# Sums over partitions by the tensor engine, taken 32 columns wide instead of one or two

## The chip, the cores and the metric

The kernel runs on one core of one Trainium2 chip. The metric is the time on the device in microseconds (us), the median of several runs. One more execution of each kernel is taken with the hardware profiler. The engines are named as the profile names them: PE is the tensor engine (PEld its weight loads), DVE the vector engine, ACT the scalar engine, POOL GpSimd, SP the engine that issues most of the DMAs.

## What is computed

The reference puts two transformer blocks behind one another, on 512 tokens of width 1024, all in float32. Cut to what matters here:

```python
# block 1
mod = silu(c) @ mod_w + mod_b                      # six vectors of 1024
h = rmsnorm(x, norm1_g) * (1 + sc1) + sh1          # a sum over 1024 features for each token
x = x + g1 * (mixed(h) @ w_out)                    # attention with forget gates, and pooling
h = rmsnorm(x, norm2_g) * (1 + sc2) + sh2
x = rmsnorm(x + g2 * conv_ffn(h), final_g)
# block 2
h = rms_norm(x, ln1_g); proj = h @ w_in
aq, ak = rms_norm(heads(aq), q_norm_g), rms_norm(heads(ak), k_norm_g)   # a sum over 64 features of a head
attn = rms_norm(neighbourhood_attention(aq, ak, av), attn_out_g)
dn = rms_norm(gated_delta_rule(l2_norm(q), l2_norm(k), v, ...), out_norm_g) * silu(z)   # sums over 128 features of a head
x = x + concat([attn, dn]) @ w_out
x = x + hierarchical_moe(rms_norm(x, ln2_g), ...)  # 64 experts, two for each token
```

## The kernel before

Up to the end of the mixer of the second block, activations lie with features on the 128 partitions and the 512 tokens along the free axis (`xT` is eight tiles of 128x512). A sum over features is then a sum over partitions, and the tensor engine takes it: a 128x128 piece of the squares is loaded as weights, a column of ones is streamed through it, and the result is one column of PSUM with a token's sum on each partition. Four such matmuls cover 512 tokens. In float32 one matmul of the program is two instructions of PE, each with its own weight load.

These places take such sums. `gemv_done` (L268 to L275) turns the accumulated products of a modulation vector into eight columns. `shift_share` (L277 to L289) does it for the shift's share of a projection, two columns. `ColSums.done` (L308 to L312) does it for squares that POOL has added up, `ColSumsPE.done` (L327 to L333) for squares that PE has added up into 32 equal rows of four quarters; there the column is `w32`, which holds 1/32. `head_norm` (L726 to L748) uses a selector of two columns (`hsel`), one for each head of 64 features. `dn_q_out` (L1033 to L1041) and `scan_out` (L1188 to L1209) take sums over the 128 features of a head. Behind each a DVE instruction reads the few columns from PSUM, mostly followed by a power -1/2 on POOL and, where the row is needed along the free axis, by four transposes on PE (`row_bcast`, L348).

The big projections are matmuls of 128x512 at L177 to L179 (three products of split fp32 operands); between the projections stand the attention heads (L485, L508, L526), the levels of a triangular inverse (`levels`, L1079 to L1111, its 128-column matmuls at L1098) and the scan (L1153 to L1186). From about 1060 us on the experts run, with their matmuls at L1728 and L1757.

The order of PE's instructions is fixed when the program is built: a planner orders the work of each engine by its place in the code, readiness and its own costs, save where `manual_schedule` pins PE's order (the attention heads, the router and the experts). So a sum can stand among matmuls of a projection or of an attention head, and `gemv_done` of a vector can run long before the code's last user of it.

Of the kernel before, what the change touches and what calls it, by code (L numbers as in the profile page):

```python
# [9 lines left out]
F32 = mybir.dt.float32  # L10
# [4 lines left out]
AF = mybir.ActivationFunctionType  # L15
ALU = mybir.AluOpType
# [5 lines left out]
EPS = 1e-6  # L22
# [67 lines left out]
def hybrid_kernel(ctx, tc, A, out, dbg=None):  # L90
    nc = tc.nc
# [7 lines left out]
    cp = pool("const")  # L99
# [8 lines left out]
    vec = cp.tile([128, _NV], F32, name="vec")  # L108
    cst = cp.tile([128, _NC], F32, name="cst")

    def V(name, i=0, n=1):
        o, _ = _VEC[name]
        return vec[:, o + i:o + i + n]

    def C(name):
        if name in _CST:
            o, n = _CST[name]
            return cst[:, o:o + n]
        o, n = _CST2[name]
        return cst2[:, o:o + n]  # L120

    ident = C("ident")
    ones32 = cp.tile([128, 32], F32, name="ones32")
    w32 = cp.tile([128, 1], F32, name="w32")
    zb = cp.tile([128, 128], BF16, name="zb")
    nhalf = cp.tile([128, 8], F32, name="nhalf")
    modT = cp.tile([128, 48], F32, name="modT")
    gs = cp.tile([128, 16], F32, name="gs")
    nc.vector.memset(ones32, 1.0)
    nc.vector.memset(w32, 1.0 / 32.0)  # L130
    nc.gpsimd.memset(zb, 0.0)
    nc.vector.memset(nhalf, -0.5)

# [134 lines left out]
    def gemv_done(u, acc):  # L268

        if acc is None:  # L270
            return
        p = ps("gv", "gvt")
        for j in range(8):
            nc.tensor.matmul(p[:, j:j + 1], acc[j // 4][:, j % 4 * 128:j % 4 * 128 + 128], ones32[:, 0:1], start=True, stop=True)
        nc.vector.tensor_tensor(modT[:, u * 8:u * 8 + 8], p[:, 0:8], V("mod_b", u * 8, 8), op=ALU.add)  # L275

    def shift_share(w_raw, sh0, pool):  # L277

        sw = pool.tile([128, 256], F32, name="sw")
        for k in range(8):  # L280
            sk, wk = modT[:, sh0 + k:sh0 + k + 1], w_raw[k // 4][:, k % 4, :]
            if k == 0:
                nc.vector.tensor_scalar(sw, wk, sk, None, op0=ALU.mult)
            else:
                nc.vector.scalar_tensor_tensor(sw, wk, sk, sw, op0=ALU.mult, op1=ALU.add)
        p = ps("gv", "pqb")
        for m in range(2):
            nc.tensor.matmul(p[:, m:m + 1], sw[:, m * 128:m * 128 + 128], ones32[:, 0:1], start=True, stop=True)
        return p  # L289


    class ColSums:
# [15 lines left out]
        def done(self):  # L308
            pt = ps(self.tag, "cst")
            for t in range(4):  # L310
                nc.tensor.matmul(pt[:, t:t + 1], self.a[:, t * 128:t * 128 + 128], ones32[:, 0:1], start=True, stop=True)
            return pt[:, 0:4]  # L312

    class ColSumsPE:

# [10 lines left out]

        def done(self):  # L327
            part = sp_.tile([128, S], F32, tag="tmp", name="part", bufs=4)
            nc.scalar.activation(part, self.p, AF.Copy)
            pt = ps(self.tag, "cst")  # L330
            for t in range(4):
                nc.tensor.matmul(pt[:, t:t + 1], part[:, t * 128:t * 128 + 128], w32, start=True, stop=True)
            return pt[:, 0:4]  # L333

    def col_sums(srcs, tag="pc"):
        cs = ColSumsPE(len(srcs), tag)
# [257 lines left out]
    with ExitStack() as st:  # L594
# [13 lines left out]
        for m in range(2):  # L608
            a = fp.tile([128, S], F32, tag="act", name="a_first", bufs=2)
# [6 lines left out]
        for third, n in enumerate((8, 8, 6)):  # L616
            ah, al = [], []
            for jj in range(n):
                j = off + jj
                if j == 7:  # L620
                    gemv_done(5, acc5)
                p = proj(A["wup"][j], hh, hl, tag=("pb", "mm")[j % 2]) if j else p_first
                cv = []
                for m in range(2):
                    ci = j + 22 * m
                    c = fp.tile([128, S], F32, tag=f"cv{m}", name=f"cv{m}", bufs=2)
# [99 lines left out]
    def head_norm(pp, gain):  # L726

        pt = ps("pa", "hn")
        aa = []
        for m in range(2):  # L730
            a = slot("cv", "a", 6)
            nc.scalar.activation(a, pp[m], AF.Copy, scale=gain)
            aa.append(a)
            sq = slot("cv", "sq", 6)
            nc.scalar.activation(sq, pp[m], AF.Square)
            for t in range(4):
                o = m * 8 + t * 2
                nc.tensor.matmul(pt[:, o:o + 2], sq[:, t * 128:t * 128 + 128], C("hsel"), start=True, stop=True)
        v, r = (sp_.tile([128, 2] + d, F32, tag=f"hn{i}", name="hnv", bufs=1 + i) for i, d in enumerate(([4, 2], [2, 4])))
        pv = pt[:, 0:16].rearrange("p (m t e) -> p m t e", m=2, t=4)  # L740
        for m in range(2):
            nc.vector.tensor_tensor(v[:, m], pv[:, m], rr2.unsqueeze(2).to_broadcast([128, 4, 2]), op=ALU.mult)
        nc.vector.tensor_scalar(v, v, 1.0 / 64, EPS, op0=ALU.mult, op1=ALU.add)
        for m in range(2):
            nc.gpsimd.tensor_tensor(v[:, m], v[:, m], nhalf.rearrange("p (t e) -> p t e", t=4), op=ALU.pow)
            nc.vector.tensor_tensor(r[:, m].rearrange("p e t -> p t e"), v[:, m], rr.unsqueeze(2).to_broadcast([128, 4, 2]),
                                    op=ALU.mult)
        return aa, r  # L748
# [284 lines left out]
    def dn_q_out(c):  # L1033
        for h in (2 * c, 2 * c + 1):
            sq = tmp("sq")
            nc.scalar.activation(sq, qT[h], AF.Square)
            pt = ps("pb", "pqs")
            for t in range(4):
                nc.tensor.matmul(pt[:, t:t + 1], sq[:, t * 128:t * 128 + 128], ones128[:, 0:1], start=True, stop=True)
            nc.vector.tensor_scalar(qs[:, h * 4:h * 4 + 4], pt[:, 0:4], 128 * EPS, 128 * EPS * EPS,  # L1040
                                    op0=ALU.mult, op1=ALU.add)  # L1041

    vT = {}
# [144 lines left out]
    def scan_out(po, tag):  # L1188
        pt = ps(tag, "pst")
        a = sp_.tile([128, 2, 4], F32, tag="sa", name="sa", bufs=1)  # L1190
        r = sp_.tile([128, 2, 4], F32, tag="sr", name="sr", bufs=1)
        h0 = min(po)
        da = {}
        for h in po:
            so, da[h] = tmp("so"), tmp("da")
            nc.scalar.activation(so, po[h], AF.Square)
            nc.vector.scalar_tensor_tensor(da[h], po[h], V("dng"), zs[h], op0=ALU.mult, op1=ALU.mult)
            for t in range(4):
                i = (h - h0) * 4 + t
                nc.tensor.matmul(pt[:, i:i + 1], so[:, t * 128:t * 128 + 128], ones128[:, 0:1], start=True, stop=True)  # L1200
        nc.vector.scalar_tensor_tensor(a, pt[:, 0:8].rearrange("p (h t) -> p h t", h=2), 1.0 / 128,
                                       qs[:, h0 * 4:h0 * 4 + 8].rearrange("p (h t) -> p h t", h=2),
                                       op0=ALU.mult, op1=ALU.add)
        nc.gpsimd.tensor_tensor(r, a, nhalf.rearrange("p (h t) -> p h t", h=2), op=ALU.pow)
        for h in po:
            R = row_bcast(r[:, h - h0], "pb")
            nc.vector.tensor_tensor(da[h], da[h], R, op=ALU.mult)
            new_mix2(4 + h)
            split_h(mixh[4 + h], mixl[4 + h], da[h])  # L1209
# [715 lines left out]
```

## Time and profile before

| | us |
|---|---|
| median of 3 runs | 1554.95 |
| lowest and highest run | 1553.94, 1559.04 |
| profiled execution, its own time | 1553.21 |
| profiled execution, span from the first to the last instruction | 1551.3 |

PE is busy 95% of the span, DVE 54%, ACT 33%, POOL 16%. The mean granted clock of PE is 0.972 of its full speed. In the page's 40 slices a granted clock below full speed stands in the first slices, around the middle of the span and at the change to the experts. The chain that ended last lies on PE for 76% of the span.

"Granted clock" is the clock that PE was allowed in a stretch, as a share of 2.4 GHz; 0.5 is 1.2 GHz. In a timeline row the first number is the start in us from the start of the span, the second the time from the first start to the last end of the instructions that the row merges. Ends of matmuls are modelled and a matmul's row holds its way through the array, so that the step from one start to the next tells more of its cost than its duration.

### The profile page before, as it was taken

What the parts mean: (1) busy time and instruction counts of PE and PEld (TensorE: products, weight loads), DVE (VectorE), ACT (ScalarE), POOL (GpSimd) and SP (SyncE); (2) the same over time, 40 slices, a digit from 0 to 9 for tenths busy, and PEclk for the clock granted to TensorE, in tenths of its full rate; (3) what the DMA queues carried; (4) which work ended last, traced back from release to release, by engine and by line L of the source; (5) the groups of instructions that cost most, each with busy time, mean ns of one, the idle gap of its engine ahead of it and who ended that gap; (6) DMA issues with size and microseconds to landing.
All of it is one profiled execution on the core that took longest, in us unless ns stands there. A gap on an engine that the chain in (4) does not pass through costs nothing.

```text
span 1551.3 us, 20448 instructions
## 1 busy us (share of the span) xinstructions
PE 1467.0 (95%) x7500; PEld 1012.8 (65%) x7500; DVE 842.6 (54%) x1724; ACT 516.1 (33%) x981; POOL 251.6 (16%) x317
## 2 busy tenths in 40 slices
PE   6899999999999999998889999997999999999997
PEld 3766686888888887876667788884444444444443
DVE  3778776653564457266797666564333333233234
ACT  4554434441442345254334434422311111111111
POOL 0242021000000004323562330102100000000000
PEclk9989999999999999998989999997999999999999
DMA  8753143332222223353333131567999999999995
GB/s 334 244 201 122 60 145 109 103 101 94 96 96 95 95 82 99 101 171 102 85 116 77 30 92 50 196 220 295 421 418 424 425 423 424 424 424 424 423 424 185
DMA packets 82573, 327.69 MB, mean 211 GB/s; under 512 B 18086, under 2 KB 21798, under 8 KB 58144
## 3 DMA queue, kind: packets, MB, share of 16 engines
q1 hardware_dynamic: 80736, 321.63, 55.4%
q0 software_dynamic: 1728, 4.66, 0.8%
q8 instruction: 61, 1.00, 0.3%
q14 instruction: 48, 0.39, 0.1%
HBM read 319.42 MB, written 8.47 MB: 211 GB/s over the span
## 4 chain that ended last, share of the span: by engine, by line
PE 76%; DVE 10%; DMA 4%; issue 3%; POOL 3%; ACT 2%; SPq 1%; DVEq 0%; POOLq 0%; ACTq 0%
PE pgu L1728 14%; PE pj L177 10%; PE pj L179 10%; PE pj L178 10%; PE pd L1757 7%; PE pkept L1775 2%; PE pkept L1776 2%; PE pcmb L1775 2%; PE pcmb L1776 2%; DVE wlo L171 2%; DMA graw<-in_modw_dram 1%; DVE cv L875 1%; PE pS L485 1%; DMA xg<-xs,tok_of 1%; DVE E L950 1%
## 5 line engine op out<-in xcount | busy, mean ns | idle before, releaser
L177 PE MATMUL pj<-hh,whi 128*128 128x512 f32 x640 | 259.2, 406 | 16.1 <-ACT cn L869 7.7
L179 PE MATMUL pj<-hh,wlo 128*128 128x512 f32 x640 | 257.2, 403 | 4.8 <-DVE wlo L171 4.8
L178 PE MATMUL pj<-hl,whi 128*128 128x512 f32 x640 | 257.1, 402 | 0.5 <-DVE hl L200 0.5
L1728 PE MATMUL pgu<-wgu,xw 128*64 128x512 f32 x1024 | 227.1, 596 | 0.1
L171 DVE TENSOR_TENSOR wlo<-wraw,whi 128x1024 fp32r<-128x1024 f32 (+4 forms) x122 | 148.4, 1218 | 47.6 <-ACT whi L170 44.5
L170 ACT ACTIVATE whi<-wraw 128x1024 fp32r<-128x1024 f32 (+4 forms) x122 | 125.0, 1027 | 136.3 <-PE pj L178 119.2
L1728 PEld LDWEIGHTS pgu<-wgu,xw 128*64 128x64 f32 x1024 | 70.4, 137 | 139.3 <-issue 137.9
L177 PEld LDWEIGHTS pj<-hh,whi 128*128 128x128 f32 x640 | 123.5, 193 | 48.8 <-ACT cn L869 10.2
L179 PEld LDWEIGHTS pj<-hh,wlo 128*128 128x128 f32 x640 | 123.7, 194 | 34.6 <-DVE wlo L171 5.3
L178 PEld LDWEIGHTS pj<-hl,whi 128*128 128x128 f32 x640 | 123.8, 193 | 26.0 <-issue 1.2
L1734 DVE SCALAR_TENSOR_TENSOR hid<-pgu,agt,sg 128x256 f32<-128x256 f32 x32 | 15.5, 484 | 194.0 <-ACT sg L1732 194.0
L1732 ACT ACTIVATE sg<-pgu,agt 128x256 f32<-128x256 f32 x32 | 15.2, 476 | 305.1 <-PE pgu L1728 305.1
L1757 PE MATMUL pd<-wd,hT 128*64 128x512 f32 x512 | 115.5, 593 | 0.4 <-ACT xgT L1580 0.4
L1779 DVE TENSOR_TENSOR xr<-xr,pcmb 128x512 f32<-128x512 f32 x128 | 82.2, 683 | 28.7 <-PE pcmb L1776 28.7
L306 POOL TENSOR_TENSOR acc<-acc,sq 128x512 f32<-128x512 f32 x21 | 33.7, 1623 | 391.6 <-ACT sq L305 391.3
L198 DVE SCALAR_TENSOR_TENSOR og<-pd,agt,og 128x512 fp32r<-128x512 f32 x64 | 48.0, 750 | 79.6 <-ACT og L194 79.6
L1719 POOL COPY xw<-xgT 128x512 f32 x56 | 32.9, 616 | 353.8 <-PE pgu L1728 343.7
L1757 PEld LDWEIGHTS pd<-wd,hT 128*64 128x64 f32 x512 | 36.2, 137 | 72.3 <-issue 63.1
L179 PE MATMUL pj<-ah,wlo 128*128 128x512 f32 x176 | 69.3, 394 | 0.0
L177 PE MATMUL pj<-ah,whi 128*128 128x512 f32 x176 | 69.3, 394 | 0.0
L178 PE MATMUL pj<-al,whi 128*128 128x512 f32 x176 | 69.3, 394 | 0.0
L194 ACT ACTIVATE og<-pd,agt 128x512 fp32r<-128x512 f32 x64 | 44.0, 688 | 75.3 <-PE pd L1757 74.2
(455 smaller groups left out, 2630.3 us busy)
## 6 DMA issues: line engine op xcount, KB each, us to landing
wgu<-in_egu_dram SPq DMA_DIRECT2D x128, 1024.0 KB
wd<-in_ed_dram SPq DMA_DIRECT2D x62, 1024.0 KB
graw<-in_modw_dram SPq DMA_DIRECT2D x48, 512.0 KB
wraw<-in_wup_dram SPq DMA_DIRECT2D x42, 512.0 KB
wraw<-in_win_dram SPq DMA_DIRECT2D x38, 512.0 KB
wraw<-in_wdn_dram SPq DMA_DIRECT2D x20, 512.0 KB
wraw<-in_wout_dram SPq DMA_DIRECT2D x16, 512.0 KB
E<-gscr SPq DMA_DIRECT2D x16, 256.0 KB
```

The costliest lines, as they stand in the source:

```text
L170: nc.scalar.activation(hi, raw, AF.Copy)
L171: nc.vector.tensor_tensor(lo, raw, hi.bitcast(F32), op=ALU.subtract)
L177: nc.tensor.matmul(p, whi, hh, start=first, stop=False)
L178: nc.tensor.matmul(p, whi, hl, start=False, stop=False)
L179: nc.tensor.matmul(p, wlo, hh, start=False, stop=last)
L194: nc.scalar.activation(hi, src, AF.Identity, scale=scale, bias=0.0 if bias is None else bias)
L198: nc.vector.scalar_tensor_tensor(lo, src, scale, hi.bitcast(F32), op0=ALU.mult, op1=ALU.subtract)
L1728: nc.tensor.matmul(gu[64 * i:64 * i + 64, :], xw[:, j, 64 * i:64 * i + 64], wts.gu[e][j], start=(j == 0), stop=(j == 7))
L1757: nc.tensor.matmul(pd[64 * i:64 * i + 64, :], hT[:, j, 64 * i:64 * i + 64], wts.d[e][:, j, n * 512:n * 512 + 512], start=(j == 0), stop=(j ...
L1775: nc.tensor.matmul(pc, OT[:, ts], a, start=(n == 1 or start), stop=False, skip_group_check=(n == 0))
L1776: nc.tensor.matmul(pc, OT[:, ts], b, start=False, stop=(n == 1 or stop), skip_group_check=(n == 0))
L1779: nc.vector.tensor_tensor(v, v, pc, op=ALU.add)
```

## The change

All sums over partitions named above stream 32 equal columns instead of one: `ones32`, a 128x32 tile of ones that was there, takes the place of its own first column, of the first column of `ones128`, and of `w32`, which is removed with its memset. The scale 1/32 of `w32` moves into the copy on ACT ahead of it. The selector of two columns is repeated 16 times by its access pattern. Each sum now has 32 columns of PSUM instead of one, and a new helper, `wide`, gives the readers a view of every 32nd column. Number and order of the matmuls in the code stay as they were.

```diff
+    def wide(p, n):
+        return p[:, 0:32 * n].rearrange("p (n c) -> p n c", c=32)[:, :, 0]
...
-    w32 = cp.tile([128, 1], F32, name="w32")
...
-    nc.vector.memset(w32, 1.0 / 32.0)
...
 # gemv_done
-            nc.tensor.matmul(p[:, j:j + 1], acc[j // 4][:, j % 4 * 128:j % 4 * 128 + 128], ones32[:, 0:1], start=True, stop=True)
-        nc.vector.tensor_tensor(modT[:, u * 8:u * 8 + 8], p[:, 0:8], V("mod_b", u * 8, 8), op=ALU.add)
+            nc.tensor.matmul(p[:, 32 * j:32 * j + 32], acc[j // 4][:, j % 4 * 128:j % 4 * 128 + 128], ones32, start=True, stop=True)
+        nc.vector.tensor_tensor(modT[:, u * 8:u * 8 + 8], wide(p, 8), V("mod_b", u * 8, 8), op=ALU.add)
...
 # shift_share
-            nc.tensor.matmul(p[:, m:m + 1], sw[:, m * 128:m * 128 + 128], ones32[:, 0:1], start=True, stop=True)
-        return p
+            nc.tensor.matmul(p[:, 32 * m:32 * m + 32], sw[:, m * 128:m * 128 + 128], ones32, start=True, stop=True)
+        return wide(p, 2)
...
 # ColSums.done
-                nc.tensor.matmul(pt[:, t:t + 1], self.a[:, t * 128:t * 128 + 128], ones32[:, 0:1], start=True, stop=True)
-            return pt[:, 0:4]
+                nc.tensor.matmul(pt[:, 32 * t:32 * t + 32], self.a[:, t * 128:t * 128 + 128], ones32, start=True, stop=True)
+            return wide(pt, 4)
...
 # ColSumsPE.done
-            nc.scalar.activation(part, self.p, AF.Copy)
+            nc.scalar.activation(part, self.p, AF.Copy, scale=1.0 / 32)
...
-                nc.tensor.matmul(pt[:, t:t + 1], part[:, t * 128:t * 128 + 128], w32, start=True, stop=True)
-            return pt[:, 0:4]
+                nc.tensor.matmul(pt[:, 32 * t:32 * t + 32], part[:, t * 128:t * 128 + 128], ones32, start=True, stop=True)
+            return wide(pt, 4)
...
 # head_norm
-                o = m * 8 + t * 2
-                nc.tensor.matmul(pt[:, o:o + 2], sq[:, t * 128:t * 128 + 128], C("hsel"), start=True, stop=True)
+                o = (m * 4 + t) * 32
+                nc.tensor.matmul(pt[:, o:o + 32], sq[:, t * 128:t * 128 + 128],
+                                 C("hsel").unsqueeze(1).to_broadcast([128, 16, 2]), start=True, stop=True)
...
-        pv = pt[:, 0:16].rearrange("p (m t e) -> p m t e", m=2, t=4)
+        pv = pt[:, 0:256].rearrange("p (m t c) -> p m t c", m=2, t=4)[:, :, :, 0:2]
...
 # dn_q_out
-                nc.tensor.matmul(pt[:, t:t + 1], sq[:, t * 128:t * 128 + 128], ones128[:, 0:1], start=True, stop=True)
-            nc.vector.tensor_scalar(qs[:, h * 4:h * 4 + 4], pt[:, 0:4], 128 * EPS, 128 * EPS * EPS,
+                nc.tensor.matmul(pt[:, 32 * t:32 * t + 32], sq[:, t * 128:t * 128 + 128], ones32, start=True, stop=True)
+            nc.vector.tensor_scalar(qs[:, h * 4:h * 4 + 4], wide(pt, 4), 128 * EPS, 128 * EPS * EPS,
...
 # scan_out
-                nc.tensor.matmul(pt[:, i:i + 1], so[:, t * 128:t * 128 + 128], ones128[:, 0:1], start=True, stop=True)
-        nc.vector.scalar_tensor_tensor(a, pt[:, 0:8].rearrange("p (h t) -> p h t", h=2), 1.0 / 128,
+                nc.tensor.matmul(pt[:, 32 * i:32 * i + 32], so[:, t * 128:t * 128 + 128], ones32, start=True, stop=True)
+        nc.vector.scalar_tensor_tensor(a, wide(pt, 8).rearrange("p (h t) -> p h t", h=2), 1.0 / 128,
```

## Rows read from the trace of the kernel before

**Rows 1.** The page: span, busy time by engine, the chain by engine

```profile
span 1551.3 us, 20448 instructions
...
PE 1467.0 (95%) x7500; PEld 1012.8 (65%) x7500; DVE 842.6 (54%) x1724; ACT 516.1 (33%) x981; POOL 251.6 (16%) x317
...
PE 76%; DVE 10%; DMA 4%; issue 3%; POOL 3%; ACT 2%; SPq 1%; DVEq 0%; POOLq 0%; ACTq 0%
```

**Rows 2.** PE's groups by line and shape: count | busy us, mean ns | idle before

```profile
L738 PE MATMUL hn<-cst,sq 128*128 128x2 f32 x64 | 9.5, 270 | 5.8 <-ACT sq L735 5.7
...
L984 PE MATMUL kk<-kT 128*128 128x128 f32 x32 | 4.3, 276 | 0.0
L551 PE MATMUL ppool<-ud,pw 128*128 128x512 f32 x8 | 4.1, 592 | 0.0
```

**Rows 3.** Timeline of PE, 842 to 856 us: start, us, line, count

```profile
845.75 1.06 PE L1098 MATMUL lvW<-U,DD 128*128 128x128 f32 x8
846.77 1.05 PE L1039 MATMUL pqs<-ones,sq 128*128 128x1 f32 x8
...
848.40 1.05 PE L1039 MATMUL pqs<-ones,sq 128*128 128x1 f32 x8
849.31 1.55 PE L1098 MATMUL lvY<-DD,U 128*128 128x128 f32 x8
850.65 1.92 PE L1098 MATMUL lvQ<-YY,NX 128*128 128x128 f32 x8
```

**Rows 4.** Stretches: PE, PEld, DVE, ACT, POOL busy; granted clock, DMA share, GB/s

```profile
621.20:624.60 3.40, 2.89 (x22) 2.38 (x20) 1.39 (x4) 0.00 (x0) 2.05 (x2) 1.00 0.00 0
624.60:628.00 3.40, 3.40 (x10) 2.72 (x10) 2.48 (x5) 0.04 (x1) 2.93 (x11) 0.50 0.60 192
...
846.40:849.80 3.40, 3.40 (x28) 2.90 (x27) 1.60 (x5) 2.12 (x6) 1.84 (x2) 1.00 0.35 124
849.80:853.20 3.40, 3.40 (x18) 3.40 (x18) 2.57 (x4) 1.19 (x2) 0.21 (x1) 0.51 0.00 0
853.20:856.60 3.40, 3.40 (x31) 3.11 (x30) 2.50 (x4) 0.00 (x0) 0.53 (x1) 0.99 0.00 0
```

**Rows 5.** Timeline of PE, 618 to 650 us, at the sums of L311

```profile
622.08 1.05 PE L311 MATMUL cst<-ones,acc 128*128 128x1 f32 x8 [0.51 <-POOL acc L306]
...
623.78 0.95 PE L311 MATMUL cst<-ones,acc 128*128 128x1 f32 x8
624.59 0.77 PE L178 MATMUL pj<-hl,whi 128*128 128x512 f32 x1
```

**Rows 6.** Timelines of PE at four idle gaps; in brackets the idle time before

```profile
18.38 1.11 PE L351 MATMUL rb<-cst,rsr 128*128 128x128 f32 x4 [2.32 <-POOL rsr L345]
...
94.70 0.70 PE L485 MATMUL pS<-kT,zq 64*128 64x256 f32 x2 [2.51 <-DVE mx L493]
...
95.77 2.98 PE L274 MATMUL gvt<-ones,gacc 128*128 128x1 f32 x14
...
243.56 1.05 PE L311 MATMUL cst<-ones,acc 128*128 128x1 f32 x8 [2.32 <-POOL acc L306]
...
708.88 1.87 PE L738 MATMUL hn<-cst,sq 128*128 128x2 f32 x8 [5.20 <-ACT sq L735]
```

**Rows 7.** Stretches as in rows 4, behind the four gaps

```profile
17.00:24.00 7.00, 5.62 (x52) 2.90 (x56) 1.54 (x2) 0.00 (x0) 1.32 (x1) 0.51 1.03 411
...
95.00:106.00 11.00, 11.00 (x38) 7.60 (x36) 5.78 (x31) 4.63 (x12) 2.30 (x2) 0.53 0.56 206
...
245.00:250.00 5.00, 5.00 (x18) 4.02 (x17) 2.28 (x4) 1.34 (x2) 0.92 (x1) 0.66 0.00 0
...
710.00:720.00 10.00, 10.00 (x32) 8.44 (x33) 4.55 (x11) 2.22 (x5) 4.84 (x11) 0.50 0.37 92
```

**Rows 8.** DVE's reads of PSUM behind transposes (L229) and sums (L275), by line and shape

```profile
L229 DVE TENSOR_TENSOR modT<-gvt,vec 128x8 f32<-128x8 f32 x3 | 0.5, 166 | 2.4 <-PE gvt L226 2.4
...
L275 DVE TENSOR_TENSOR modT<-gvt,vec 128x8 f32<-128x8 f32 x3 | 0.5, 160 | 1.3 <-PE gvt L274 1.3
```

## The prediction

> **What bounds the kernel now.** I read the page first, for the engine that the chain follows: the tensor engine (PE) is busy 95% of the 1551.3 us and carries 76% of the chain that ended last [rows 1]. So a microsecond taken from or given to PE in a stretch where it has no idle time moves the end by about as much, and what a slower engine beside it does is mostly cover. I read next the groups of PE instructions by line and shape, for what the edited matmuls cost today: 64 instructions at L738 [rows 2], and by the same view 48 at L274, 32 each at L1039, L1200 and L311, 8 each at L332 and L288, 224 in all. Each fp32 matmul of the program is two instructions, so 112 matmuls. Last I read the timeline and the stretches around each group of sums, for what they wait for, how far apart they start, and above all at which granted clock PE runs before and after them.
>
> The reader should see two things there. A sum of one column is not cheap: eight instructions at L1039 start at 846.77 us and what follows the second such group starts 0.91 us after it (848.40 to 849.31) [rows 3], that is about 0.11 us an instruction, the same step as eight instructions with 128 columns (lvW, 845.75 to 846.77, 1.02 us) [rows 3]. And the clock falls right behind sums: in 846.4 to 849.8 us PE is busy all of 3.40 us at a granted clock of 1.00, in the next 3.40 us it is still busy all the time, and the granted clock is 0.51 [rows 4], the lower of its two levels, 1.2 GHz against 2.4 GHz. The sums of the two normalisations before the second block (L311) show the same: two groups from 622.08 to 624.59 [rows 5], granted clock 1.00 in 621.2 to 624.6 and 0.50 in 624.6 to 628.0 [rows 4].
>
> **The change part by part.**
>
> *The width itself.* 224 instructions stream 32 columns instead of one (two at L738). The trace has one-column and two-column sums and 128-column matmuls with the same 128x128 fp32 weights, and 32 lies between. By means, the 128-column L984 takes 276 ns and the two-column L738 270 ns [rows 2]: 6 ns for 126 columns. The step from start to start is the same 0.11 us for both [rows 3]. So the weight load sets the step and the columns run under it: cost of the step 0, lower bound 0 (nothing is taken out that could give time), upper bound below under the rivals. What is left is that the last matmul of a group ends later for its reader. There are 20 places where a reader waits (by the code three vectors of the modulation, two shift shares, five normalisations, four head norms, four query sums, two of the scan). At 6 ns each that is 0.1 us, at the slope between L984 and the 512-column L551 (592 less 276 ns over 384 columns, 0.82 ns a column, 31 columns, 26 ns) [rows 2] it is 0.5 us. I take 0.1 us, since 128 columns is the nearer row.
>
> *The readers.* DVE now reads every 32nd column of the bank instead of neighbours. The trace has both ways on the same shape: L229 reads every 32nd column of a bank and takes 166 ns, L275 reads neighbours and takes 160 ns [rows 8]. Cost 6 ns at most a place, counted at 0. Bounds 0 to 0.1 us over 20 places.
>
> *Moved arithmetic and the removed tile.* The 1/32 goes from the column of weights into the scale of a copy that ScalarE makes anyway, and a memset at the start goes; neither is on the chain, which enters the start by the loads of x. If that cover is gone they cost or give under 0.1 us. No DMA, queue or wait is added, and no instruction is added to or taken from PE. The two-column selector (L738) becomes a repeated read of the same two columns. I cost it as a 32-column read. No row shows such a narrow repeat as a moving operand, so its bounds are those of the width.
>
> *The clock.* This is the only term of size. A fall costs what its stretch loses: 3.40 us busy at 0.51 does 1.73 us of full-speed work, a loss of 1.67 us, and 3.40 us at 0.50 loses 1.70 us [rows 4]. The rows around the first one check it: the groups that start at 849.31 and 850.65 us show 1.55 and 1.92 us against 1.06 us for lvW before [rows 3], 1.35 us on two groups with a third still slow. Which falls would go? In six places low clock stands beside sums. At two of them the sums are what PE does before the fall: at 846.77 to 849.3 us there is no idle time at all, at 622.08 to 624.59 us there is 0.51 us [rows 3, 5]. There the columns that pass rise most, so there I let the fall go: 1.67 + 1.70 = 3.37 us. At the other four a real gap of PE comes first: 2.32 us ahead of 18.38, 2.51 us ahead of 94.70, 2.32 us ahead of 243.56 and 5.20 us ahead of 708.88 us [rows 6]. A few wider sums don't fill a gap, so I let these stay. Bounds of the clock term: 0 to all six. PE is busy without a break in both low stretches [rows 4], and what is late next is PE itself, so the gain isn't taken by another engine at once.
>
> The Trainium skill, page "TensorE: Matmul & The Clock Gate", section "Why this matters for your kernels", puts falls of the clock down to idle gaps of PE between bursts of matmuls. By that alone the stretch before 849.8 us, which has none, would not fall, and wider sums would save nothing. The row differs: the clock falls there, so I go by the row. By the page the sum is +0.1 us, by the rows -3.3 us.
>
> *Sum.* -3.37 + 0.1 = -3.27 us on the profiled execution's 1553.21 us (span 1551.3 and 1.9 around it), 1549.9 us. The median of the runs shown, 1554.95, stands 1.74 us above that execution, so the median is forecast at 1551.7 us.
>
> **The rivals.**
>
> *B, the columns don't count enough.* The falls at 624.6 and 849.8 us stay, or as many come elsewhere. For it: 32 columns under a step that has room for 128 is still mostly weight loading. Against it: 853.2 to 856.6 us, as full of small matmuls with as many weight loads but of 128 columns, keeps a granted clock of 0.99 [rows 4], and the stretch that fell differs from it by its narrow sums. Time: +0.1 to +0.5 us, 1555.1 to 1555.5.
>
> *C, more falls go.* The stretches behind the gaps shrink too. Losses there: 17 to 24 us at 0.51, 3.4 us; 95 to 106 at 0.53, 5.2; 245 to 250 at 0.66, 1.7; 710 to 720 at 0.50, 5.0 [rows 7], 15.3 us together. For it: after 95.77 and 708.88 us the sums themselves run at the low clock (eight instructions take 1.87 us) [rows 6] and may be what holds it there. Against it: the gaps. With a typical one of these, 3.4 us, on top of the forecast: -6.7 us, 1548.3; with all, 1536.4.
>
> *D, the columns are not hidden.* If the weight load can't run beside the matmul before it, each instruction grows by 31 columns at 0.82 ns, 26 ns [rows 2], over 224 instructions 5.7 us, and PE is the bound. Then the change is slower: 1560.7 if the falls stay, 1557.4 if the two go. It decides from 15 ns an instruction on, where the cost passes the 3.37 us saved. The place to see it is the four head norms (L738), 64 instructions. Against it stand the equal steps of one and 128 columns [rows 3]. The Trainium skill, same page, section "Part 3: Packing small matmuls", says that weights load beside a running matmul only when the row groups differ, which here they don't; by that D would hold. The trace disagrees: the step stays 0.11 us with 128 columns.
>
> *E, the order of PE changes.* The program's order on PE is fixed when it is built, by a plan that weighs costs: the first modulation sums stand in the code behind all four head pairs (L580) and run among the logits of the first at 95.77 us [rows 6]. A sum that the plan takes for longer may be put elsewhere. The place is there and at the sums of 708.88 us; a group of eight that lands in a low stretch ahead of chain work costs 1.87 - 1.05 = 0.8 us [rows 5, 6], a new fall 1.7 us. It decides with three new falls, about +5 us: 1560. It can also help, which is part of C.
>
> **How the numbers follow.** About 0.3% (4.7 us) is what a measurement of this kernel can tell from no change. Forecast A, 0.42, with its own range 1550.0 to 1553.5. B 0.25, C 0.22, D 0.05, E 0.06. Below 1550.3 us lie nearly all of C (0.21) and some of A (0.09): faster 0.30. Above 1559.6 us lie half of D and E: slower 0.09. Same: 0.61. For the range I leave out the deep half of C and most of D and E: 1546 to 1557.5.
>
> **What would show it.** Right: eight 32-column sums still about 0.9 us from start to start; granted clock near 1.00 behind 624.6 and 849.8 us; the gaps of 2.3 to 5.2 us with low clock behind them as now. Wrong: a step above 0.13 us (D); the two falls there as before (B); low clock also gone behind a gap (C); groups of sums at other places in the order of PE (E).

## The result and the profile after

| | us, median (from to) | ratio to before |
|---|---|---|
| kernel before | 1555.01 (1553.94 to 1559.04) | 1 |
| changed kernel | 1573.61 (1572.40 to 1580.44) | 1.0131 [1.0096, 1.0166] |
| its profiled execution | 1572.4, span 1570.6 | |

The change costs 18.6 us by the medians, 15 to 26 us by the interval of the ratio; the forecast was 1551.7, the range 1546 to 1557.5.

The page of the changed kernel: span, busy time by engine, the chain by engine.

```profile
span 1570.6 us, 20450 instructions
...
PE 1475.9 (94%) x7500; PEld 1014.4 (65%) x7500; DVE 846.0 (54%) x1723; ACT 517.6 (33%) x981; POOL 255.3 (16%) x317
...
PE 74%; DVE 11%; DMA 6%; issue 3%; POOL 3%; ACT 3%; SPq 0%; DVEq 0%; POOLq 0%; ACTq 0%
```

Against [rows 1] PE has as many instructions and is busy 8.9 us longer; its idle time went from 84.3 to 94.7 us. So half of the loss is PE at a worse pace, half is PE waiting. Next the groups of the edited matmuls by line and shape (count | busy us, mean ns | idle before).

```profile
L740 PE MATMUL hn<-cst,sq 128*128 128x32 f32 x64 | 9.7, 301 | 5.8 <-ACT sq L737 5.7
...
L987 PE MATMUL kk<-kT 128*128 128x128 f32 x32 | 4.3, 276 | 0.0
```

The head norms went from 9.5 to 9.7 us over 64 instructions [rows 2]: 0.2 us where rival D needed 1.7. The mean of one rose by 31 ns (270 to 301), but that is its way through the array and not the step to the next. The width is not what costs. What moved is seen in PE's timeline (start, us, line, count; two windows).

```profile
98.51 3.04 PE L276 MATMUL gvt<-ones,gacc 128*128 128x32 f32 x14
...
165.25 0.41 PE L276 MATMUL gvt<-ones,gacc 128*128 128x32 f32 x2
165.49 0.48 PE L179 MATMUL pj<-hh,whi 128*128 128x512 f32 x1
```

In [rows 6] 14 instructions of the same group stand at 95.77 us, and the last two of the 16 follow by 100.1 us. Now the last two, the eighth sum of the third modulation vector, run 67 us after the others, among the logits of a later head pair. That sum reads one of the two buffers of the tag "gacc", so the buffer isn't free until 165 us, and the fifth vector's first product (ScalarE) starts at 166.56 instead of 106.32 us. ScalarE in the kernel before, then in the changed kernel:

```profile
106.32 0.71 ACT L259 ACTIVATE gacc<-graw,cact 128x512 f32<-128x512 f32 x1
...
166.56 0.72 ACT L261 ACTIVATE gacc<-graw,cact 128x512 f32<-128x512 f32 x1
```

GpSimd shows the hole (start, us, line; in brackets the idle time before).

```profile
104.40 1.04 POOL L264 TENSOR_TENSOR graw<-graw,cact 128x512 f32<-128x512 f32 x1 [0.72 <-DMA graw<-in_modw_dram]
166.59 0.11 POOL L544 MEMSET us<- 128x16 f32 x1 [61.15 <-DVE ud L550]
...
185.88 1.04 POOL L264 TENSOR_TENSOR graw<-graw,cact 128x512 f32<-128x512 f32 x1 [13.88 <-DVE gacc L259]
187.00 1.59 POOL L267 TENSOR_TENSOR gacc<-gacc,graw 128x512 f32<-128x512 f32 x1
```

The products that before were spread over 106 to 156 us run, most of them, at 182 to 202 us, where DVE makes the pooled sums that PE's next matmuls need. The stretch from 185 to 204 us in the kernel before, then the same and the next in the changed kernel (columns as in [rows 4]):

```profile
185.00:204.00 19.00, 19.00 (x100) 15.23 (x96) 12.01 (x21) 6.01 (x8) 0.56 (x5) 1.00 0.16 55
...
185.00:204.00 19.00, 14.21 (x71) 10.40 (x69) 18.95 (x16) 4.42 (x8) 14.99 (x12) 0.93 0.57 194
204.00:216.00 12.00, 10.49 (x41) 7.19 (x41) 7.07 (x16) 1.57 (x3) 0.34 (x3) 0.83 0.23 65
```

In the changed kernel DVE is busy 18.95 of 19.00 us and PE 14.21, and the granted clock is 0.93 and then 0.83. The longest wait of PE from 160 to 218 us names the place (us in total, times, longest); the kernel before has no wait there:

```profile
PE ppool L553 <- DVE ud L551: 5.8, 1, 5.8
```

The lag of the changed kernel by landmarks that both traces have, each the start of the last instruction of a line: pooled-head matmuls (L551 of before) 199.6 to 212.2, +12.6 us; the second block's transposes (L700) 667.5 to 682.2, +14.6; neighbourhood logits (L815) 974.9 to 993.8, +18.9; the router's matmuls (L1622) 1059.3 to 1076.8, +17.4; the last gate-and-up matmul (L1728) 1526.7 to 1545.9, +19.2. Most of it arises by 212 us, some 4 us between 667 and 975, and 2 us, evenly, under the experts. A second profile of the kernel before lies 2.7, 5.9, 2.5, 3.1 and 2.6 us behind the first at the same five places, so that of the steps up to 1059 us only the first is by itself clear of what two executions of one kernel differ by; that later places cost something too rests on n_shgv and w_hn below.

### The profile page after: what moved, and what is told of

It reads as the page before. It is cut to its first block, busy times and chain, and to the rows that moved or that the text cites. A ratio compares the mean times of both kernels' runs of the same rounds, so it can differ in the third digit from the quotient of the medians.

```text
span 1570.6 us, 20450 instructions
## 1 busy us (share of the span) xinstructions
PE 1475.9 (94%) x7500; PEld 1014.4 (65%) x7500; DVE 846.0 (54%) x1723; ACT 517.6 (33%) x981; POOL 255.3 (16%) x317
## 4 chain that ended last, share of the span: by engine, by line
PE 74%; DVE 11%; DMA 6%; issue 3%; POOL 3%; ACT 3%; SPq 0%; DVEq 0%; POOLq 0%; ACTq 0%
PE pgu L1731 14%; PE pj L179 10%; PE pj L181 10%; PE pj L180 10%; PE pd L1760 7%; DMA graw<-in_modw_dram 3%; PE pkept L1778 2%; PE pkept L1779 2%; PE pcmb L1779 2%; PE pcmb L1778 2%; DVE wlo L173 2%; DVE cv L878 1%; PE pS L487 1%; DMA xg<-xs,tok_of 1%; DVE E L953 1%
## 5 line engine op out<-in xcount | busy, mean ns | idle before, releaser
L173 DVE TENSOR_TENSOR wlo<-wraw,whi 128x1024 fp32r<-128x1024 f32 (+4 forms) x122 | 148.0, 1215 | 51.9 <-ACT whi L172 48.8
```

The lines of the kernel that those rows point to most:

```text
L173: nc.vector.tensor_tensor(lo, raw, hi.bitcast(F32), op=ALU.subtract)
```

## The experiments

All ratios are to the kernel before, timed beside each kernel on the same chip (its medians there were 1553.9 to 1554.4 us); differences in us are differences of these medians unless a trace is named. "Order" is the order of instructions on each engine, which the plan sets when the program is built.

### Width or order

**wide_old_order** keeps the changed kernel and pins every engine to the order of before: at the end of the trace each instruction gets an edge, without a semaphore, to the one ahead of it on its engine in that order (a list of some 9,600 numbers).

```diff
+    made = {i.name: i for i in tc.nc.cur_bb.bb.instructions}
...
+            if last is not None:
+                tc.add_manual_dep(i, last.name, mybir.DependencyInfo(mybir.DependencyClass.NoSync, mybir.DependencyReason.DATA),
+                                  reason="the order of before")
+            last = i
```

> All sums 32 columns wide, but every engine's instructions in the order of the kernel before. Theory O (the added 19 us come from another order, which the planner chose because it takes wider sums for longer): 1551 to 1555 us, that is the time of before less up to 3.4 us for two falls of the clock that wider sums avert. Theory W (the width itself costs on the chip, by longer steps on PE or by the clock): 1568 to 1575 us, as the changed kernel.

Measured: 1554.64 us, 1.0002 [0.9990, 1.0014]. **narrow_new_order** is the reverse: every sum as narrow as before, pinned in the same way to the changed kernel's order.

```diff
-            nc.tensor.matmul(p[:, 32 * j:32 * j + 32], acc[j // 4][:, j % 4 * 128:j % 4 * 128 + 128], ones32, start=True, stop=True)
+            nc.tensor.matmul(p[:, j:j + 1], acc[j // 4][:, j % 4 * 128:j % 4 * 128 + 128], ones32[:, 0:1], start=True, stop=True)
...
+    keep_order(tc)
```

> All sums one or two columns wide as before, but every engine's instructions in the order of the changed kernel. Theory O: 1573 to 1577 us, the time of the changed kernel plus what narrower sums lose at the clock. Theory W: 1554 to 1556 us, as before.

Measured: 1573.54 us, 1.0132 [1.0116, 1.0149], span 1571.2. With 1-column sums the whole loss is there, with 32-column sums in the old order none of it. The order carries it.

### The late eighth sum

**wide_edge** ties the eighth sum (I-1702) ahead of a projection matmul (I-1038), so that it runs with the other seven.

```diff
+    tc.add_manual_dep(made["I-1038"], "I-1702",
+                      mybir.DependencyInfo(mybir.DependencyClass.NoSync, mybir.DependencyReason.DATA), reason="order")
```

> The changed kernel with one ordering edge more: the eighth sum of the third modulation vector, which it runs at 165.25 us, is put ahead of the projection matmul that follows the other seven near 101 us. Theory O1 (this one late matmul holds the accumulators, so the fifth vector's products come 74 us later and collide with the work before the output projection): 12 us come back, 1559 to 1563 us. If the lag has many small causes or is of the width: 1570 to 1575 us.

Measured: 1569.05 us, 1.0100 [1.0084, 1.0117]: a miss. The edge gave back 4.5 us, not 11 to 15; adding it also moved other work, and its trace is 6.5 us late at 107 us and 15.4 at the end. The loss behind the late sum is gone all the same (see the end of this part). **narrow_edge** is the opposite on the kernel before: nothing wide, that one sum held back behind a later pair's logits (I-1559).

```diff
+    tc.add_manual_dep(made["I-1702"], "I-1559",
+                      mybir.DependencyInfo(mybir.DependencyClass.NoSync, mybir.DependencyReason.DATA), reason="order")
```

> The kernel before with the same eighth sum, narrow as it was, held back by one edge to the place where the changed kernel has it, behind the second matmul of a later head's logits. Theory O1: 1565 to 1569 us, 10 to 14 us more than before with nothing made wider. If the lag is of the width or of many small causes: 1554 to 1557 us.

Measured: 1568.56 us, 1.0100 [1.0083, 1.0118]. One narrow matmul held back to row 640 of PE's order, with what the plan then moves beside it, costs 14 us. **only_shgv** lets the plan do it by itself: wide sums in `gemv_done` and `shift_share` only, the other sums as before, as in this hunk.

```diff
-                nc.tensor.matmul(pt[:, t:t + 1], part[:, t * 128:t * 128 + 128], w32, start=True, stop=True)
+                nc.tensor.matmul(pt[:, t:t + 1], part[:, t * 128:t * 128 + 128], ones32[:, 0:1], start=True, stop=True)
```

> The kernel before with the wide sums only in gemv_done and shift_share (56 of the 112 matmuls); all later sums narrow. Nothing pins the order, so the plan sets it anew, and the eighth sum of the third modulation vector falls at the same late row of PE's order (640) as in the changed kernel. If that one sum and what goes with it carry the loss: 1566 to 1570 us, about what the narrow kernel with that sum alone held back took (1568.6), with a lag of +6 to +14 us from 216 us on and no further step at 780 to 1000 us. If the loss needs the later sums too: 1556 to 1561.

Measured: 1572.42 us, 1.0125 [1.0104, 1.0146], 2 us over the upper end expected. The early 56 wide sums are enough for nearly all of the loss. **wide_hp** marks the changed kernel's group as urgent.

```diff
-        gemv_done(2, acc2)
+        with tc.high_priority():
+            gemv_done(2, acc2)
```

> The changed kernel with the sums of the third modulation vector marked urgent for the plan: all eight now stand together at row 293 of PE's order, ahead of where before has them (358). If only the late eighth sum matters here: the lag at 216 us goes from +12 to 0 or +3 us, what is left are the later places (+9 in the run with the later sums wide alone), 1561 to 1565 us. If the earlier place stalls PE behind products that aren't ready: 1568 or more.

Measured: 1565.40 us, 1.0074 [1.0048, 1.0100]: a little over the first range; some 8 us of the loss are back. Its trace is still some 6 us late at 205 us. **narrow_late_copy** asks why a late sum costs so much. The eighth sum and the addition that reads it stay as late as in narrow_edge, all else keeps the order of before, but the sum reads a copy, so that the buffer comes free early.

```diff
+            late = ap.tile([128, 128], F32, name="late")
+            nc.scalar.activation(late, acc[1][:, 384:512], AF.Copy)
...
+                nc.tensor.matmul(p[:, 7:8], late, ones32[:, 0:1], start=True, stop=True)
```

> All sums narrow, every engine in the order of before, but the eighth sum of the third modulation vector and the addition that reads it come as late as in narrow_edge (row 640 of PE's order), and that sum reads a copy of its 128 columns (one more copy on ScalarE), so that the accumulators come free as early as before and the fifth vector's products stand where before has them. If the held accumulators are what the late sum costs: 1555.5 to 1558 us (with 2.0 us for the moved weight buffers). If the late sum itself, or its reader, costs it: 1566 to 1569 us, as narrow_edge.

Measured: 1556.40 us, 1.0014 [0.9999, 1.0028]. The copy and the fifth vector's first product on ScalarE (start, us, line):

```profile
108.15 0.30 ACT L366 ACTIVATE late<-gacc 128x128 f32<-128x128 f32 x1
108.48 0.72 ACT L350 ACTIVATE gacc<-graw,cact 128x512 f32<-128x512 f32 x1
```

and the same two stretches as above, in this kernel:

```profile
185.00:204.00 19.00, 19.00 (x97) 14.52 (x95) 11.45 (x25) 6.10 (x11) 0.56 (x5) 1.00 0.22 71
204.00:216.00 12.00, 12.00 (x62) 10.21 (x61) 9.69 (x15) 4.50 (x6) 1.69 (x1) 1.00 0.62 207
```

PE is busy throughout at full clock, DVE 11.45 us instead of 18.95, GpSimd 0.56 instead of 14.99. The sum itself runs at 167.61 us here, later than in the changed kernel, and costs nothing as such. Against narrow_edge this kernel differs in two things, the copy and the pinned order of all the rest, so it doesn't part the buffer from the rest of the plan by itself. The time from the first to the last pooled-head matmul, by the traces, does:

| kernels | eighth sum at | first to last pooled-head matmul |
|---|---|---|
| before, wide_old_order | 100 us | 32.3 us |
| wide_edge, wide_hp | 101, 79 us | 32.1, 31.1 us |
| narrow_late_copy (sum late, buffer free early) | 168 us | 32.3 us |
| changed, narrow_new_order, only_shgv | 165, 165, 167 us | 44.4, 44.5, 45.5 us |
| narrow_edge | 158 us | 44.7 us |

Wide or narrow, in three plans, the stretch takes 12 to 13 us more when the late sum holds the buffer, and in no other of these kernels. It holds a buffer that the next vector's products wait for, and these then fall where DVE has work that PE waits for. From 200 to 220 us PE is busy 14.15 us in the changed kernel and all the time in wide_edge (changed kernel first):

```profile
200.00:220.00 20.00, 14.15 (x57) 10.23 (x58) 15.03 (x23) 4.71 (x7) 5.20 (x8) 0.83 0.36 124
...
200.00:220.00 20.00, 20.00 (x93) 15.68 (x92) 14.10 (x25) 6.94 (x9) 2.40 (x3) 1.00 0.45 149
```

So wide_edge and wide_hp win these 12 us back; what they lose, 6 to 7 us ahead of 175 us and a few at the later places, is of their own orders.

### The later places

**n_shgv** is the complement of only_shgv: those two helpers narrow again, the other 56 sums wide.

```diff
-            nc.tensor.matmul(p[:, 32 * m:32 * m + 32], sw[:, m * 128:m * 128 + 128], ones32, start=True, stop=True)
-        return wide(p, 2)
+            nc.tensor.matmul(p[:, m:m + 1], sw[:, m * 128:m * 128 + 128], ones32[:, 0:1], start=True, stop=True)
+        return p
```

> The complement: the changed kernel with gemv_done and shift_share narrow again, the other 56 matmuls wide. The sums of the modulation stand in the order of before. If the early sum carries the loss: 1554 to 1560 us, with steps of +2 to +6 us only at the normalisations and the query and head sums between 620 and 1000 us. If the loss comes from the later places: 1566 to 1570.

Measured: 1563.44 us, 1.0050 [1.0033, 1.0067], above the 1554 to 1560 expected. Three kernels then widen one place each, all else as before: the head norms (**w_hn**), the query sums (**w_dq**), the scan's output sums (**w_so**); w_dq's hunk stands for all.

```diff
-                nc.tensor.matmul(pt[:, t:t + 1], sq[:, t * 128:t * 128 + 128], ones128[:, 0:1], start=True, stop=True)
+                nc.tensor.matmul(pt[:, 32 * t:32 * t + 32], sq[:, t * 128:t * 128 + 128], ones32, start=True, stop=True)
```

> The kernel before with the head norms alone wide (32 matmuls, two columns to 32), the 1/32 in the copy, the tile w32 gone; the plan orders anew, and the order differs from PE's row 2440 on, at the head norms of the second block. If these carry what the later sums cost: 1562 to 1564 us. If not: 1556 to 1557, before plus 2.0 us for the moved weight buffers.

> The kernel before with the query sums alone wide (16 matmuls), the 1/32 in the copy, w32 gone; the order differs from PE's row 3016 on, among the neighbourhood heads. If these carry what the later sums cost: 1562 to 1564 us. If not: 1556 to 1557.

> The kernel before with the sums of the scan's output alone wide (16 matmuls), the 1/32 in the copy, w32 gone; the order differs from PE's row 3394 on. If these carry what the later sums cost: 1562 to 1564 us. If not: 1556 to 1557.

Measured: w_hn 1564.36 us, 1.0060 [1.0042, 1.0077]; w_dq 1554.45, 1.0004 [0.9989, 1.0020]; w_so 1558.82, 1.0029 [1.0012, 1.0046]. The head norms carry what the later sums cost, by themselves as much as all together. In the trace of w_hn the projection's matmuls are 4.3 us late at 759 us of before, while DVE's work for the scan is level (+0.3); GpSimd's first clearing of the scan's blocks is 9.5 us late (820.9 us in before) and its last neighbourhood bias 23 us (929.8 to 952.8). PE's lag is -0.8 us at 940 us of before and 8.0 at 980: in 940 to 960 and 980 to 1000 us of its own trace the granted clock is 0.93 and 0.91, against 1.00 in before. Which single wait makes it was not followed further. w_dq lies 1.5 us under the lower of its ranges. w_so lies between its two; its trace is already 5 us late at 625 us, ahead of where its order differs, and the second profile of the kernel before is as late there (4.4 to 4.8 us), so that it shows no loss of its own for certain. The parts don't add up to the whole: each kernel's order is a plan of its own.

### The two microseconds under the experts

From the fifth to the last pair of experts (27 pairs) the first gate-and-up matmul (L1728) starts at 1129.26 and 1520.22 us in before, 14.480 us a pair, and at 1146.66 and 1539.40 us in the changed kernel, 14.546. Over 31 pairs that is 2.0 us.

```profile
1129.26 7.09 PE L1728 MATMUL pgu<-wgu,xw 128*64 128x512 f32 x32
1520.22 7.09 PE L1728 MATMUL pgu<-wgu,xw 128*64 128x512 f32 x32
...
1146.66 7.09 PE L1731 MATMUL pgu<-wgu,xw 128*64 128x512 f32 x32
1539.40 7.09 PE L1731 MATMUL pgu<-wgu,xw 128*64 128x512 f32 x32
```

**before_again** is the kernel before, unchanged.

> The kernel before itself, for a second profile of it. In the first one each pair of experts takes 14.480 us at a steady pace, in the five profiles of other kernels since, the changed one's among them, 14.546 us; over 31 pairs that is 2.0 us. If the pace belongs to the execution and not to the kernel, it is 14.54 to 14.55 us here, the median 1553 to 1556 us and the profiled span 1552 to 1555; if the edits slow that stage, it is 14.48 us again.

Measured: 14.480 us a pair again, 1555.09 us, 1.0005 [0.9992, 1.0018], span 1554.0. The pace belongs to the kernel and not to the execution. **wide_old_again** repeats wide_old_order.

> The changed kernel's widths in the order of before once more, with more rounds, beside the kernel before on the same chip. Clock term worth nothing to the end: 1553.5 to 1555.5 us, ratio 1.000. Clock term worth the 2.0 us by which its profile was ahead at 1064 us: 1552 to 1553.5 us, ratio 0.9985 to 0.9990. As first forecast, 3.3 us: ratio 0.998.

Measured: 1554.08 us, 1.0000 [0.9985, 1.0014], 14.546 us a pair, although its experts start at 1062.5 us, ahead of before (1064.3 and 1066.8 in its two profiles). What all the slower kernels share is the missing tile `w32`: without it most tiles lie 32 bytes lower in their partition. **wide_old_pad** is wide_old_order with the room kept.

```diff
-    ones32 = cp.tile([128, 32], F32, name="ones32")
+    ones32 = cp.tile([128, 33], F32, name="ones32")[:, 0:32]
```

> The changed kernel's widths in the order of before, with the tile of ones 33 columns wide (one column unused), so that every tile behind it lies where it lies in the kernel before; without the tile w32 they had moved 32 bytes towards the start of their partition. If the moved tiles slow the experts' stage: 14.480 us a pair instead of 14.546, 2.0 us less than wide_old_order, 1552.0 to 1553.0 us, ratio 0.9985 to 0.999. If the pace hangs on the widths or the pinned order instead: 14.546 us a pair and 1554 to 1555 us.

Measured: 14.480 us a pair; 1551.70 us, 0.9988 [0.9974, 1.0002], the least of all kernels here, not surely less than before. **narrow_old_less** is before without `w32`, all sums narrow, its order kept by itself.

```diff
-    w32 = cp.tile([128, 1], F32, name="w32")
-    nc.vector.memset(w32, 1.0 / 32.0)
...
-            nc.scalar.activation(part, self.p, AF.Copy)
+            nc.scalar.activation(part, self.p, AF.Copy, scale=1.0 / 32)
```

> The kernel before without the tile w32 alone: all sums narrow, the order the same as before, the 1/32 in the scale of the copy. If the removed tile slows the experts' stage: 14.546 us a pair, 2.0 us more than before, 1556 to 1557 us, ratio 1.001 to 1.0015. If not: 14.480 us a pair, 1554 to 1555.

Measured: 14.546 us a pair; 1556.19 us, 1.0021 [1.0007, 1.0035]. The removed tile alone costs the 2 us. **wide_old_wgu** (first line changed) moves the weight buffers and all behind them back, **wide_old_og** (second) only what lies behind the weight buffers, the scaled outputs `og` among it; both otherwise as wide_old_order.

```diff
-    ssum, sa, rn = lt("ssum", (128, 4)), lt("sa", (128, 4)), lt("rn", (128, 4))
+    ssum, sa, rn = lt("ssum", (128, 4)), lt("sa", (128, 4)), lt("rn", (128, 12))[:, 0:4]
...
-            iota = lt("iota", (128, S))
+            iota = lt("iota", (128, S + 8))[:, 0:S]
```

> As wide_old_order, but only the last tile ahead of the experts' weight buffers is 32 bytes longer, so that the weight buffers (wgu) and what follows them lie where they lie in the kernel before, and all that is ahead of them stays moved. If the place of the weight buffers sets the pace: 14.480 us a pair, 1552.0 to 1553.0 us. If it is another of the moved tiles: 14.546 us a pair, 1554 to 1555.

> As wide_old_order, but the 32 bytes stand behind the weight buffers: wgu stays moved (38688 in its partition), the scaled outputs og lie where the kernel before has them (122688). If og sets the pace: 14.480 us a pair and 389 ns for a pcmb matmul. If wgu sets it: 14.546 us and 396 ns.

Measured: 14.480 us a pair in both; 1553.15 us, 1.0003 [0.9989, 1.0016], and 1553.66, 0.9996 [0.9976, 1.0017]. In wide_old_og the weight buffers are still moved, so they are not it, though wide_old_wgu alone would fit them and two of the expectations above name them. PE's groups from 1200 to 1480 us (count | busy us, mean ns | idle before), first wide_old_order:

```profile
L1861 PE MATMUL pcmb<-og,OT 128*128 128x512 f32 x77 | 30.5, 396 | 0.0
L1860 PE MATMUL pcmb<-og,OT 128*128 128x512 f32 x76 | 30.1, 396 | 0.0
L1861 PE MATMUL pkept<-og,OT 128*128 128x512 f32 x76 | 30.0, 394 | 0.0
```

then wide_old_og:

```profile
L1860 PE MATMUL pcmb<-og,OT 128*128 128x512 f32 x80 | 31.1, 389 | 0.0
L1861 PE MATMUL pcmb<-og,OT 128*128 128x512 f32 x80 | 31.1, 389 | 0.0
L1861 PE MATMUL pkept<-og,OT 128*128 128x512 f32 x77 | 30.1, 391 | 0.0
```

Eight pcmb matmuls a pair at 7 ns and four pkept at 3 ns make 68 ns, and the pace differs by 66. They read `og` as their moving data; of the tiles behind the weight buffers it is the only one that these matmuls read and that moved. It lies at byte 122688 of a partition in before, at 122656 without the tile. **wide_pad** puts the room back into the changed kernel in its own order.

> The changed kernel in its own order with the tile of ones 33 columns wide, so that all tiles lie where they lie in the kernel before. If the two losses add: 14.480 us a pair and 1571 to 1572 us, 2.0 less than the 1573.6 of the changed kernel. If the pace follows the order: 14.546 us and 1573 to 1574.

Measured: 14.480 us a pair; 1571.59 us, 1.0113 [1.0078, 1.0148]. So the change splits into about 17.5 us of order, with what the width gives or takes at the clock in it, and 2.0 us of moved tiles.

## Why the prediction was wrong

**The width itself, and rival D: right, but for the tail.** In the order of before the groups of query sums of wide_old_order (start, us, line, count) keep the step of [rows 3]:

```profile
849.78 1.08 PE L1124 MATMUL pqs<-ones,sq 128*128 128x32 f32 x8
850.69 1.14 PE L1183 MATMUL lvY<-DD,U 128*128 128x128 f32 x8
851.66 1.06 PE L1183 MATMUL lvQ<-YY,NX 128*128 128x128 f32 x8
```

0.91 us for eight instructions, with 32 columns as with one. The Trainium skill, page "TensorE: Matmul & The Clock Gate", section "Part 3: Packing small matmuls", has weights load beside a running matmul only when the row groups differ; this step speaks against that once more. The tail of 6 ns was misread: it set the 128-column L984 against an L738 whose mean holds instructions at the low clock. Like with like, a 32-column sum takes 25 to 31 ns more, as at L1200 of before and the same place in wide_old_order (count | busy us, mean ns | idle before):

```profile
L1200 PE MATMUL pst<-ones,so 128*128 128x1 f32 x32 | 3.8, 246 | 0.0
...
L1285 PE MATMUL pst<-ones,so 128*128 128x32 f32 x32 | 3.9, 272 | 0.0
```

Over 20 places that is about 0.5 us, the other end of the bounds. The readers were right: 148 to 166 ns at L277 against 160 [rows 8].

**"No DMA, queue or wait is added": the step that failed.** It held for the instructions and not for their order. The plan placed seven sums where they were and one 67 us later, and that sum carried a wait that stands in no diff: the fifth vector's products wait for the buffer it reads. Rival E had the cause, and both its places, the sums at 95.77 and at 708.88 us, were right ones: the first is the third modulation vector, the second the head norms. But it was given a chance of 0.06 and about 5 us, because its price was sought in the clock (0.8 and 1.7 us a fall) instead of in what a late sum holds. The late sum that holds its buffer costs 12 us (32.3 to 44.7 us between the pooled-head matmuls in narrow_edge), the same sum late with its buffer free costs nothing (narrow_late_copy), and the head norms' new order cost w_hn 10 us, 2 of them the tile. What stayed on the same engines in the same amount was taken to stay in the same place.

**"The removed tile, under 0.1 us": mis-sized.** It measured 2.0 us, not by its memset but by the addresses of what lies behind it. The prediction had no term for addresses.

**The clock term, -3.37 us: mis-sized.** Its size came from a single execution, which had both falls. Narrow sums are not always followed by one. Behind the query sums of the kernel before the clock fell in its first profile [rows 4] and not in its second. Timeline of before_again there:

```profile
853.23 1.05 PE L1039 MATMUL pqs<-ones,sq 128*128 128x1 f32 x8
854.14 1.14 PE L1098 MATMUL lvY<-DD,U 128*128 128x128 f32 x8
855.12 1.06 PE L1098 MATMUL lvQ<-YY,NX 128*128 128x128 f32 x8
```

and of narrow_old_less, with the stretches ahead of the fall and behind it (columns as in [rows 4]):

```profile
849.41 1.05 PE L1041 MATMUL pqs<-ones,sq 128*128 128x1 f32 x8
850.32 1.96 PE L1100 MATMUL lvY<-DD,U 128*128 128x128 f32 x8
852.07 1.91 PE L1100 MATMUL lvQ<-YY,NX 128*128 128x128 f32 x8
...
846.00:850.30 4.30, 4.30 (x37) 3.81 (x36) 2.40 (x5) 3.46 (x9) 1.33 (x2) 1.00 0.53 185
850.30:853.80 3.50, 3.50 (x19) 3.50 (x19) 2.88 (x5) 0.60 (x1) 0.73 (x1) 0.52 0.00 0
```

The same sums in the same order: no fall in one execution, 0.52 in the other, with PE busy 4.30 of 4.30 us ahead of it. The Trainium skill, page "TensorE: Matmul & The Clock Gate", section "Why this matters for your kernels", puts such falls down to idle gaps; here, as in [rows 4], none stands ahead of it. All twenty profiles together bear the mechanism out: at the two places of the 3.37 us, whatever the order, a fall begins with the end of the narrow sums (0.9 us before it to 0.5 us behind it) in 4 of 10 profiles at the normalisations and in 4 of 9 at the query sums, and with the end of the wide ones in none of 10 and none of 11. With 1.70 and 1.67 us a fall that makes the two worth about 1.4 us on average, an estimate, not 3.37. Why one execution falls and the next does not is not shown. Rival C did not come: in all five profiles of wide sums in the old order the clock is still low at 0.5 behind the gaps of 18, 95, 244 and 709 us. (C's first loss, 3.4 us in 17 to 24 us, counts idle time too; by the 5.62 us that PE was busy it is 2.8.)

The mean granted clock over the whole span hardly differs: 0.972, 0.974, 0.977 and 0.976 in four profiles with narrow sums in the order of before, 0.978, 0.976, 0.976, 0.972 and 0.975 in five with wide ones, 0.0006 on average or 0.9 us. By the times, wide against narrow gives 0.9996 (mean of the three kernels with `og` in its old place) against 1, and 1.0001 (the two with it moved) against 1.0021 and 1.0014. So the gain lies between nothing and some 3 us; the times don't tell it closer.

**The sum.** With these sizes it would have been: width +0.5, clock about -1.4, moved tiles +2.0, order +17.3 (narrow_new_order less narrow_old_less, both narrow and both without the tile), 18.4 us; measured 18.6. The sizes come from the experiments themselves, so that this fit tests nothing further. A, B and C all assumed the order of before, and wide_old_order, which has it, came to 1554.64 us: within the forecast's range, nearest to B.

## What to carry to other kernels

When a plan orders the program from costs, an edit that touches a cost is an edit of the order. Compare the order on each engine before any term is summed; for an instruction that may move, price the buffer it holds and the work that then lands elsewhere, not its own microsecond. Pin one kernel to the other's order to take width and order apart, and keep the addresses of what lies behind a removed tile.

## What the runs showed of the hardware

The place of a tile changes the time of the matmuls that read it: 396 against 389 ns for 512 moving columns of `og`, 32 bytes apart. 122688 is a multiple of 64 and 122656 of 32 only, but two places don't tell which property counts, and other moving tiles (hh, at 135136, also a multiple of 32 only) start 227 ns apart (median), as the pcmb readers of `og` do in its better place; in the other it is 234 (wide_old_order).

DVE beside GpSimd, timeline of DVE in the changed kernel (start, us, line):

```profile
195.00 1.77 DVE L545 TENSOR_TENSOR us<-us 128x512 f32<-128x512 f32 x1
...
199.28 1.75 DVE L545 TENSOR_TENSOR us<-us 128x512 f32<-128x512 f32 x1
...
204.92 0.69 DVE L545 TENSOR_TENSOR us<-us 128x512 f32<-128x512 f32 x1
```

The same addition takes 1.75 to 1.77 us while GpSimd runs its products (to 203.6 us) and 0.69 us after. The Trainium skill, page "SBUF — State Buffer", section "SBUF: two separate sides", says that a DVE instruction with two inputs in SBUF and a GpSimd instruction that reads SBUF shut each other out; the trace agrees. Over the ten DVE instructions that are slowed so between 185 and 204 us the added time is about 9 us, an estimate from their durations against those alone (1.45 to 1.63 against 0.74 us at L259, 1.75 to 1.77 against 0.69 at L545, 1.73 against 0.68 at L548, 2.28 against 1.22 at L173). So about half of DVE's 18.95 us was waiting for GpSimd's 15 us of work.
